# RWKV mixer: the inverse of each chunk's 64-row triangle from two 32-row substitutions and a joining product

## The chip, the cores and the metric

The kernel runs on one core of a Trainium2 chip. The metric is the device time of one execution in microseconds (us). The core's engines work side by side, each through its own queue of instructions: PE (TensorE, matrix products and transposes), DVE (VectorE), ACT (ScalarE), POOL (GpSimd), and SP, whose queue here issues nearly all DMA transfers. An instruction that waits for another engine or for a transfer holds everything behind it on its own engine.

## What is computed

One step of a hybrid decoder layer for a prompt of 512 tokens and a sample group of 8 x 8 tokens (576 columns in all), width 2048. One large projection `x @ w_in` feeds four mixers: RWKV-7, sliding-window attention, mLSTM and retention. Each mixer's output is gated and projected, the four are summed with sigmoid gates, one output projection and a layer norm follow. All in float32. The RWKV mixer has 16 heads of 64 channels and is, token by token:

```python
def step(S, inp):
    r_t, w_t, k_t, v_t, kk_t, a_t = inp
    sa = jnp.einsum('bhvk,bhk->bhv', S, -kk_t)
    S = (S * w_t[:, :, None, :] + sa[..., None] * (kk_t * a_t)[:, :, None, :]
         + v_t[..., None] * k_t[:, :, None, :])
    return S, jnp.einsum('bhvk,bhk->bhv', S, r_t)
```

Since `sa` of a token depends on the updates of the tokens before it, a chunk of 64 tokens worked at once needs the solution of a unit triangular system of 64 rows, I + M1, for each head. The kernel makes the (transposed) inverse of that triangle and multiplies with it.

## The kernel before

**Phases.** Phase 1 makes the projections and runs the four mixers one after another, RWKV (`branch_a`) first. Phase 2 makes the branch projections, phase 3 the output projection and the norm.

**The order on PE.** Projections of phase 1 are one stream. A projection is 16 steps (`dense_steps`), each of six products: the weights' and the inputs' exact high and low parts (`wh`, `wl`, `xh`, `xl`), three combinations by two column groups. `pump(n)` puts n steps into the program between a mixer's own instructions; those that a mixer asked for come first, then gates and other projections that nothing waits for. PE's instructions keep the program's order (`InOrder`), and so do POOL's. Instructions of DVE and ACT stay behind the last weight split before them (`Behind`). The splits of weights into `wh` (ACT, L1280) and `wl` (DVE, L1281) and the loads into the three `raw` buffers (SP, L1297) belong to the stream. `paced` keeps a DMA issue behind PE's work so far in the order in which the program is laid out; it is no wait at run time.

**RWKV.** Two heads (a pair) at a time, eight pairs, 9 chunks of 64 tokens each; the ninth is the sample group. For pair j+1, `prepare` makes keys, decays and the norm of the keys: their squares are summed on PE, `nr` is raised to the power -1/2 on POOL, and DVE copies it out for a transpose (`e<-nr`, `nb<-nr`). `grams` makes the chunk's products, masks them (`m1`, the tile tag `e3`) and starts the inversion. `recur` runs the chunks in order: each solve multiplies with the inverse `TT` (in the profile `TTbd`). The order is `grams(j)`, `prepare(j+1)`, 34 steps, `recur(j)`, `grams(j+1)`; before the last `recur` stand 110 steps.

**The inversion.** The 18 triangles of a pair (2 heads by 9 chunks) are stored to DRAM with one triangle per row (`m1d`, L435 and L436), and loaded seven times over, once for each of `NG` = 7 groups, so that 126 partitions hold (group, triangle) (`MU`, L443). Group g has the unknowns' rows g, g+7, g+14 and so on, ten of them (`NJ` = 10). `invert` is then a forward substitution on POOL: for each of 63 rows i one product `tmp = TU[:, :, i] * MU[i]` and one difference `TU -= tmp`, over i//7+1 of a partition's rows and 63-i columns. The result goes to DRAM (`td`, L385) and comes back with rows on partitions (`TTbd`, two loads, L390). `invert` is a generator: with each `pump` step it moves on one `yield`, so its instructions are spread over the projection steps: `ROWS_BEFORE` steps before the first row, one step a row and one more after every fifth, then `ROWS_STORE`, `ROWS_LOAD` and `ROWS_AFTER` steps around the two transfers. `recur` first takes steps until the generator has ended.

```python
S.paced(S.nc.sync.dma_start(out=td.rearrange("c a g t -> g c a t"), in_=tu[0:n]))
...
nc.sync.dma_start(out=mu[0:18 * NG], in_=m1d.unsqueeze(0).broadcast_to([NG, 18, 3072]))
S.side.append(self.invert(st, mua, mub, tu, tmp))
```

Lines that recur in the profile: L1177 is the helper that keeps the order of PE and POOL, L1193 the one of DVE and ACT; so groups are told apart by their tiles.

Of the kernel before, what the change touches and what calls it, by code (L numbers as in the profile page):

```python
# [13 lines left out]
ALU = mybir.AluOpType  # L14
# [17 lines left out]
# steps of a projection before the next one's first weights, and before its result is stored  # L32
AHEAD = 15
STORE = 6
# weights that are loaded between the pieces of x
# [53 lines left out]
def _constants():  # L89
    """Tables that depend on shapes alone."""  # L90
# [18 lines left out]
    g, jj = i // 18, np.arange(10)  # L109
    c["tinit"] = (np.arange(64)[None, None] == (g[:, None] + 7 * jj[None])[:, :, None]).astype(f).reshape(P, 640)  # L110
# [37 lines left out]

CONST = _constants()
# [4 lines left out]
NG = 7  # L154
NJ = 10
# steps of the projections put between the steps of this branch
# [11 lines left out]
# the pace of the inversion's rows, in such steps  # L168
ROWS_BEFORE = 8
ROWS_PACE = 5  # L170
ROWS_STORE = 4
ROWS_LOAD = 4
ROWS_AFTER = 3


def shift_mix(S, pool, ps, col, out, result):
    """token shift: x + (previous x - x) mu"""
# [39 lines left out]
class RwkvBranch:  # L217
    """Two heads at a time, in chunks of 64 tokens; the ninth chunk is the sample group.

    Rows of the arrays of a head pair: the even head's channels (or tokens) lie on partitions  # L220
    0..63 and the odd head's on 64..127; `ri` names the half that is not the head's own."""
# [6 lines left out]
    def __init__(self, S, pool):  # L228
# [7 lines left out]
        t = lambda name, shape: pool.tile([P] + shape, FP32, name=name)  # noqa: E731  # L236
# [27 lines left out]
    def ask(self, j):  # L264
        """the projections of a pair: keys, receptances and values (with 64 zeros on both sides)"""
        S = self.S

        def finish(n, col):
            def f(ps):
                if n == "v":  # L270
                    x = self.tile("xv", (T + 128,))
                    S.V.memset(x[:, 0:64], 0.0)
                    S.V.memset(x[:, 64 + T:], 0.0)
                    return shift_mix(S, self.pool, ps, col, x[:, 64:64 + T], x)
                x = self.tile("x" + n)
                return shift_mix(S, self.pool, ps, col, x, x)
            return f

        for n, col in (("k", 8 + j), ("r", j), ("v", 16 + j)):
            S.ask(f"a_{n}{j}", finish(n, col), 256)  # L280

    def prepare(self, j):
# [4 lines left out]
        # normalised keys  # L287
# [14 lines left out]
        # decay and learning rate  # L302
# [10 lines left out]
        # running sums of the decays' logarithms  # L313
# [31 lines left out]
        # bonus of the current token  # L345
# [14 lines left out]
        for h in range(2):  # L360
            rs = self.HALF[h]
            ch = lambda x: x[rs].rearrange("p (c t) -> p c t", c=9)  # noqa: E731
            stt(bk[rs, :, h], ch(t2), -0.5, ch(di))
            tt(bk[rs, :, 1 - h], ch(k), ch(di))
        self.st[j] = dict(r=r, kk=kk, bk=bk, bo=bo, dl=dl, vx=vx)

    def invert(self, st, mua, mub, tu, tmp):
        """forward substitution, one row of the unknowns' right side after another"""
        S, n = self.S, 18 * NG
        for _ in range(ROWS_BEFORE):  # L370
            yield 1
        for i in range(63):
            a = min(i // NG + 1, NJ)
            w = 63 - i
            row = mua[0:n, i, i + 1:64] if i < 32 else mub[0:n, i - 32, i - 31:32]
            S.tt(tmp[0:n, 0:a, 0:w], tu[0:n, 0:a, i:i + 1].to_broadcast([n, a, w]),
                 row.unsqueeze(1).to_broadcast([n, a, w]), eng=S.G)
            S.tt(tu[0:n, 0:a, i + 1:64], tu[0:n, 0:a, i + 1:64], tmp[0:n, 0:a, 0:w], ALU.subtract, eng=S.G)
            if i % ROWS_PACE == ROWS_PACE - 1:
                yield 1  # L380
            yield 1
        for _ in range(ROWS_STORE):
            yield 1
        td = S.dpool.tile([18, NJ, NG, 64], FP32, tag="td", name="td", bufs=2)
# [4 lines left out]
        for h in range(2):  # L389
            S.paced(S.nc.sync.dma_start(out=TT[self.HALF[h], :, h],  # L390
                                        in_=td[9 * h:9 * h + 9].rearrange("c a g t -> (a g) c t")[0:64]))
        for _ in range(ROWS_AFTER):
            yield 1

    def grams(self, j):
# [3 lines left out]
        for h in range(2):  # L399
            rs = self.HALF[h]  # L400
            ch = lambda x: x[rs].rearrange("p (c t) -> p c t", c=9)  # noqa: E731
            act(Z[rs, :, h, 0], ch(st["kk"]))
            act(Z[rs, :, h, self.SLOT_R[h]], ch(st["r"]))
        # products of the chunk's tokens, masked
# [4 lines left out]
        for c0, n in ((0, 4), (4, 4), (8, 1)):  # L409
# [7 lines left out]
            for h in range(2):  # L417
# [4 lines left out]
                b1 = lambda x: x.unsqueeze(1).to_broadcast([64, n, 64])  # noqa: E731  # L422
# [8 lines left out]
        # inverse of I + M1, transposed: rows (group, head, chunk), each group every seventh row  # L431
        m1d = S.dpool.tile([18, 3072], FP32, tag="m1d", name="m1d", bufs=2)
        for h in range(2):
            d = m1d[9 * h:9 * h + 9]
            nc.sync.dma_start(out=d[:, 0:2048].rearrange("c (i t) -> i c t", i=32), in_=m1[64 * h:64 * h + 32])  # L435
            nc.sync.dma_start(out=d[:, 2048:].rearrange("c (i t) -> i c t", i=32),  # L436
                              in_=m1[64 * h + 32:64 * h + 64, :, 32:64])
        mu = self.tile("MU", (3072,))
        mua, mub = mu[:, 0:2048].rearrange("p (i t) -> p i t", i=32), mu[:, 2048:].rearrange("p (i t) -> p i t", i=32)
        tu = self.tile("TU", (NJ, 64))  # L440
        tmp = self.tile("tmp", (NJ, 64))
        nc.sync.dma_start(out=tu, in_=S.I["c_tinit"].rearrange("p (a b) -> p a b", a=NJ))
        nc.sync.dma_start(out=mu[0:18 * NG], in_=m1d.unsqueeze(0).broadcast_to([NG, 18, 3072]))  # L443
        S.side.append(self.invert(st, mua, mub, tu, tmp))
        # tokens on partitions
# [30 lines left out]
        # the sample group's queries, masked to each batch  # L476
# [9 lines left out]
    def recur(self, j):  # L486
# [12 lines left out]
        two = lambda x: x.rearrange("p a b -> p (a b)")  # noqa: E731  # L499
# [29 lines left out]
        # the sample group  # L529
# [32 lines left out]
        # norm of each head (the even head's tokens on partitions 64..127)  # L562
# [26 lines left out]
def branch_b(S):  # L589
    nc, V, mm, tr, act, tt, stt, pm = S.nc, S.V, S.mm, S.tr, S.act, S.tt, S.stt, S.pm  # L590
    with S.tc.tile_pool(name="brb", bufs=1) as pool:
# [84 lines left out]
        def outputs(j, s):  # L676
            # probabilities with keys on partitions
# [29 lines left out]
        # the sample group: (KV head, query head, token) on partitions  # L707
# [46 lines left out]
def gate_rows(S, pool, dpool):  # L754
    """mLSTM gates, heads on partitions 0..7; returns the per-token rows the heads need"""
# [59 lines left out]
    # rows to every partition, by way of DRAM  # L815
# [4 lines left out]
    # tokens on partitions: [., 0:8] li - F, [., 32:40] weights of the state, [., 64:72] exp(-m)  # L820
# [20 lines left out]
def branch_c_heads(S, fmd, scd, cols):  # L841
    nc, V, mm, act, tt, stt, pm = S.nc, S.V, S.mm, S.act, S.tt, S.stt, S.pm
    with S.tc.tile_pool(name="brc", bufs=1, reuse_waits="tile") as pool:
# [4 lines left out]
        def conv(j, ps):  # L848
            """causal convolution of four taps and silu; twice its value"""
# [38 lines left out]
        for j in range(4):  # L888
# [4 lines left out]
            # row factors on every partition  # L893
# [20 lines left out]
            # keys with tokens on partitions, weighted for the state  # L914
# [23 lines left out]
            for e in range(2):  # L938
                h = 2 * j + e
                rs = slice(64 * e, 64 * e + 64)  # L940
                # weights of the scores, keys on partitions
# [31 lines left out]
                # the sample group  # L973
# [27 lines left out]
def rope(S, pool, ps, cos, sin, half, name, bufs=2):  # L1001
    """x cos + (x with its halves swapped) sin, channels on partitions"""
# [19 lines left out]
def branch_d(S):  # L1022
    nc, V, mm, act, tt, stt, pm = S.nc, S.V, S.mm, S.act, S.tt, S.stt, S.pm
    with S.tc.tile_pool(name="brd", bufs=1) as pool:
# [18 lines left out]
        for h in range(8):  # L1043
# [4 lines left out]
            # queries with their decay  # L1048
# [5 lines left out]
            # keys and values with tokens on partitions  # L1054
# [14 lines left out]
            # scores, keys on partitions  # L1069
# [12 lines left out]
            # outputs, chunk after chunk, and the states  # L1082
# [19 lines left out]
            # the sample group: one state for each batch  # L1102
# [23 lines left out]
def head_out(S, pool, o, i, h, which, den=None):  # L1126
    """norm over the head's 128 values (tokens on partitions), transposed, gain and bias"""
# [35 lines left out]
def hybrid_kernel(ctx: ExitStack, tc: tile.TileContext, I, O):  # L1163
# [3 lines left out]
    class InOrder:  # L1167
        """an engine whose instructions keep the order of the program"""
# [14 lines left out]
    class Behind:  # L1183
        """an engine whose instructions stay behind the last weight split before them"""
# [45 lines left out]
    def paced(ins):  # L1230
        """not before TensorE's work so far"""
# [35 lines left out]
    def behind_x(ins):  # L1267
        """not before the loads of x"""
# [16 lines left out]
    def dense_steps(src, nk, hi, lo, spl=SPL, order=False, first=None):  # L1285
        """[128 columns of src, T] = src^T @ (hi + lo); src [128, nk, 128] in DRAM."""
# [53 lines left out]
    # the projections of phase 1 as one stream, put between the mixers' steps: those that a  # L1340
    # mixer has asked for come first, then those that wait for nothing
# [7 lines left out]
    def step_finish(name, steps):  # L1349
        """one step of what follows a projection; False when it was the last"""  # L1350
# [14 lines left out]
    def start():  # L1365
        """the next projection, its first weights at once"""
# [26 lines left out]
    def duet():  # L1393
        """the first two projections side by side, while x comes in"""
# [20 lines left out]
    # phase 1  # L1415
# [49 lines left out]
    def rstd(pool, var, n, rows=slice(0, P), tag="rstd"):  # L1465
        """(var + eps) ** -0.5 of [rows, n]"""
# [9 lines left out]
    # phase 2: branch projections times their gates, summed in channel-major order  # L1476
# [21 lines left out]
    # the last of the projections cover the loads of the first branch  # L1498
# [8 lines left out]
    for n, i in enumerate(ORDER):  # L1507
        yh, yl = ys
        for c in range(16):
# [13 lines left out]
            if n == 3:  # L1523
                # the sample group's two parts lie side by side: one pass takes both
# [9 lines left out]
    # phase 3: output projection, residual, layer norm; tokens on partitions  # L1534
# [100 lines left out]
def device_inputs(inp):  # L1635
    """The inputs as the program reads them: the same values in another order."""
# [21 lines left out]
    # states: b h v k -> pair, (h k), b, v  # L1658
# [7 lines left out]
    # (h2 d) pair, b, v | n  # L1666
# [19 lines left out]
def returned(r):  # L1686
    """The outputs as the reference has them: the same values in another order."""
# [35 lines left out]
```

## Time and profile before

| | |
|---|---|
| three runs | 3387.62, 3391.55, 3398.9 us; median 3391.55 |
| profiled execution, first to last instruction | 3394.3 us |
| mean granted clock of PE | 0.985 |
| PE busy | 3292.9 us, 24166 instructions |
| DVE, ACT, POOL busy | 1561.2, 993.5, 696.9 us |
| POOL's two instructions of a row | 262.7 and 263.5 us, 504 of each |
| DMA | 384.67 MB, mean 113 GB/s |

The profiled execution is one more execution of the same program; its span is 0.1% above the median. In the profile's groups a line gives the engine, the operation, what is written from what (out<-in), the shapes, the count, then the busy time, the mean of one in ns, and the engine's idle time just before these instructions with what ended it. Timeline rows give start, duration, engine, operation and, in brackets, the idle time before and its releaser. Rows of windows give the stretch, its length, the busy time of PE, weight loads, DVE, ACT and POOL with counts, the mean granted clock of PE, the share of the 16 DMA engines and GB/s.

### The profile page before, as it was taken

How to read it: one execution, taken by the hardware profiler on the slowest of the kernel's cores; microseconds unless marked ns; L12 is line 12 of the kernel's file. 1: busy time of each engine (PE TensorE's matmuls, PEld its weight loads, DVE VectorE, ACT ScalarE, POOL GpSimd, SP SyncE). 2: the span in 40 equal slices, each digit the busy share in tenths (PEclk: the TensorE clock that was granted, in tenths of full speed). 3: DMA queues.
4: the chain of work that ended last, by engine and by line, in shares of the span. 5: the costliest groups of instructions: out<-in, count | busy, mean ns of one | idle time of the engine just before them, and what ended most of it. 6: DMA issues, size and time to landing. Idle time of an engine off the chain costs nothing.

```text
span 3394.3 us, 59113 instructions
## 1 busy us (share of the span) xinstructions
PE 3292.9 (97%) x24166; PEld 3160.5 (93%) x24166; DVE 1561.2 (46%) x3322; ACT 993.5 (29%) x2023; POOL 696.9 (21%) x1133
## 2 busy tenths in 40 slices
PE   8989998999899999999999999999999999999998
PEld 8979998989899899999999999999999999999886
DVE  5534454544444443334653455533343344555435
ACT  4323232323232323223443222222222222222211
POOL 0434435261708071611310000000000000000000
PEclk9989999999999999999999999999999999999999
DMA  5323232323231323334323333233333365554523
GB/s 166 110 82 108 95 115 84 113 89 111 87 106 63 115 91 107 112 101 133 93 90 107 94 96 95 88 123 119 101 102 115 97 197 184 184 171 132 171 79 106
DMA packets 174144, 384.67 MB, mean 113 GB/s; under 512 B 63704, under 2 KB 67544, under 8 KB 172272
## 3 DMA queue, kind: packets, MB, share of 16 engines
q1 hardware_dynamic: 173872, 380.88, 35.5%
q8 instruction: 190, 3.11, 0.4%
q14 instruction: 82, 0.67, 0.1%
HBM read 316.32 MB, written 58.11 MB: 110 GB/s over the span
## 4 chain that ended last, share of the span: by engine, by line
PE 73%; POOL 15%; DMA 6%; issue 3%; DVE 2%; SPq 1%; ACT 0%; POOLq 0%; ACTq 0%; DVEq 0%
PE psd L1177 45%; PE psd L1223 12%; PE pm L1177 10%; POOL TU L1177 7%; POOL tmp L1177 7%; PE pso L1223 6%; DMA MU<-m1d 3%; DMA raw<-in_wi 1%; DMA td<-TU 0%; POOL nr L1177 0%; DMA TTbd<-td 0%; DMA m1d<-e 0%; DMA raw<-in_wo 0%; DVE e L1193 0%; DVE wl L1281 0%
## 5 line engine op out<-in xcount | busy, mean ns | idle before, releaser
L1177 PE MATMUL psd<-xh,wh 128*128 128x288 f32 (+1 forms) x5472 | 1231.2, 306 | 10.1 <-ACT wh L1280 9.7
L1177 PE MATMUL psd<-xh,wl 128*128 128x288 f32 (+1 forms) x5472 | 1182.4, 297 | 31.7 <-DVE wl L1281 31.7
L1177 PE MATMUL psd<-xl,wh 128*128 128x288 f32 (+1 forms) x5472 | 1181.9, 297 | 0.0
L1281 DVE TENSOR_TENSOR wl<-raw,wh 128x512 fp32r<-128x512 f32 x812 | 595.7, 736 | 945.0 <-ACT wh L1280 928.9
L1280 ACT ACTIVATE wh<-raw 128x512 fp32r<-128x512 f32 x812 | 510.9, 631 | 1601.9 <-PE psd L1177 1218.0
L1177 PEld LDWEIGHTS psd<-xh,wl 128*128 128x128 f32 x5472 | 893.3, 190 | 33.7 <-DVE wl L1281 33.7
L1177 PEld LDWEIGHTS psd<-xh,wh 128*128 128x128 f32 x5472 | 883.4, 190 | 41.3 <-issue 14.5
L1177 PEld LDWEIGHTS psd<-xl,wh 128*128 128x128 f32 x5472 | 892.2, 190 | 0.0
L1177 POOL TENSOR_TENSOR tmp<-TU,MU 126x112 f32<-126x112 f32 (+49 forms) x504 | 262.7, 521 | 381.2 <-DMA MU<-m1d 342.9
L1177 POOL TENSOR_TENSOR TU<-TU,tmp 126x112 f32<-126x112 f32 (+49 forms) x504 | 263.5, 523 | 39.5
L1223 PE MATMUL psd<-yl,wh 128*128 128x288 f32 x1024 | 219.5, 295 | 0.0
L1223 PE MATMUL psd<-yh,wl 128*128 128x288 f32 x1024 | 219.4, 295 | 0.0
L1223 PE MATMUL psd<-yh,wh 128*128 128x288 f32 x1024 | 219.3, 295 | 0.0
L1177 POOL TENSOR_TENSOR rstd<-rstd,mhalf 128x5 f32<-128x5 f32 (+1 forms) x24 | 36.0, 1502 | 727.0 <-DVE rstd L1193 727.0
L1223 PEld LDWEIGHTS psd<-yh,wl 128*128 128x128 f32 x1024 | 164.6, 189 | 0.0
L1223 PEld LDWEIGHTS psd<-yh,wh 128*128 128x128 f32 x1024 | 164.6, 189 | 0.0
L1223 PEld LDWEIGHTS psd<-yl,wh 128*128 128x128 f32 x1024 | 164.6, 189 | 0.0
L1177 POOL TENSOR_TENSOR rs<-rs,mhalf 128x1 f32<-128x1 f32 (+1 forms) x5 | 4.5, 901 | 656.5 <-DVE rs L1193 656.5
L1177 POOL TENSOR_TENSOR smp<-Vbd,c_mrow 64x512 f32<-64x512 f32 x16 | 16.6, 1040 | 429.2 <-PE pm L1177 428.6
L1223 PE MATMUL pso<-w3h,mh 128*128 128x512 f32 x260 | 102.6, 395 | 1.4 <-ACT w3h L1193 1.4
L1223 PE MATMUL pso<-w3l,mh 128*128 128x512 f32 x260 | 103.3, 397 | 0.2 <-DVE w3l L1193 0.2
L1177 POOL TENSOR_TENSOR rsw<-rsw,c_sin 128x576 f32<-128x576 f32 x25 | 38.7, 1548 | 306.3 <-DMA rsw<-rx 306.3
(331 smaller groups left out, 2916.6 us busy)
## 6 DMA issues: line engine op xcount, KB each, us to landing
raw<-in_wi SPq DMA_DIRECT2D x342, 512.0 KB
raw<-in_wb SPq DMA_DIRECT2D x64, 512.0 KB
gd<-zs SPq DMA_DIRECT2D x64, 288.0 KB
th<-gd SPq DMA_DIRECT2D x64, 288.0 KB
raw<-in_wo SPq DMA_DIRECT2D x32, 512.0 KB
MU<-m1d SPq DMA_DIRECT2D x8, 1512.0 KB
zsd<-zs SPq DMA_DIRECT2D x32, 288.0 KB
ya<-yd SPq DMA_DIRECT2D x32, 288.0 KB
```

Of the source, the lines that this page charges most:

```text
L1177: ins = f(*a, **k).ins
L1223: PE.matmul(out=out, lhsT=lhsT, rhs=rhs, start=start, stop=stop)
L1280: a = nc.scalar.activation(out=wh, in_=src, func=ACTF.Copy)
L1281: b = nc.vector.tensor_tensor(out=wl, in0=src, in1=wh.bitcast(FP32), op=ALU.subtract)
```

## The change

The triangle of 64 rows is split into two of 32 and the block above the diagonal. Each inverse diagonal block is made by the substitution on POOL, now for 36 triangles of 32 rows: 31 rows in place of 63, `NG` = 3 groups (108 partitions), `NJ` = 11 rows in each. `m1d` has 36 rows of 1024 values, filled by four stores as before; `MU` is loaded three times over; `td` has 36 triangles; four loads bring the diagonal blocks to `TT`. The block above the diagonal stays on the chip: it is copied to `m12`, PE transposes the nine chunks of `TT` (in three groups, each with a copy to `t11` by ACT and DVE), then for each chunk and head one product of `m12` and `t11`, a copy with a change of sign to `g`, one product of `g` and the lower block, and a copy into `TT`. Between these stand `ROWS_JOIN` = 2 steps. The extra step after every fifth row is gone, `ROWS_STORE` is 3 in place of 4, `ROWS_AFTER` 4 in place of 3. Comments are taken out throughout, which moves line numbers and no instruction.

```diff
+HB = 32
+NG = 3
+NJ = 11
-NG = 7
-NJ = 10
...
-ROWS_PACE = 5
-ROWS_STORE = 4
+ROWS_STORE = 3
 ROWS_LOAD = 4
-ROWS_AFTER = 3
+ROWS_AFTER = 4
+ROWS_JOIN = 2
...
-    def invert(self, st, mua, mub, tu, tmp):
-        S, n = self.S, 18 * NG
+    def invert(self, mu, tu, tmp, m12):
+        S, n = self.S, 36 * NG
+        act, mm, tr, pm, V = S.act, S.mm, S.tr, S.pm, S.V
         for _ in range(ROWS_BEFORE):
             yield 1
-        for i in range(63):
+        for i in range(HB - 1):
             a = min(i // NG + 1, NJ)
-            w = 63 - i
-            row = mua[0:n, i, i + 1:64] if i < 32 else mub[0:n, i - 32, i - 31:32]
+            w = HB - 1 - i
             S.tt(tmp[0:n, 0:a, 0:w], tu[0:n, 0:a, i:i + 1].to_broadcast([n, a, w]),
-                 row.unsqueeze(1).to_broadcast([n, a, w]), eng=S.G)
-            S.tt(tu[0:n, 0:a, i + 1:64], tu[0:n, 0:a, i + 1:64], tmp[0:n, 0:a, 0:w], ALU.subtract, eng=S.G)
-            if i % ROWS_PACE == ROWS_PACE - 1:
-                yield 1
+                 mu[0:n, i, i + 1:HB].unsqueeze(1).to_broadcast([n, a, w]), eng=S.G)
+            S.tt(tu[0:n, 0:a, i + 1:HB], tu[0:n, 0:a, i + 1:HB], tmp[0:n, 0:a, 0:w], ALU.subtract, eng=S.G)
             yield 1
         for _ in range(ROWS_STORE):
             yield 1
-        td = S.dpool.tile([18, NJ, NG, 64], FP32, tag="td", name="td", bufs=2)
+        td = S.dpool.tile([36, NJ, NG, HB], FP32, tag="td", name="td", bufs=2)
         S.paced(S.nc.sync.dma_start(out=td.rearrange("c a g t -> g c a t"), in_=tu[0:n]))
         for _ in range(ROWS_LOAD):
             yield 1
         TT = self.TT
         for h in range(2):
-            S.paced(S.nc.sync.dma_start(out=TT[self.HALF[h], :, h],
-                                        in_=td[9 * h:9 * h + 9].rearrange("c a g t -> (a g) c t")[0:64]))
+            for b in range(2):
+                r0, c0 = 64 * h + HB * b, 18 * h + 9 * b
+                S.paced(S.nc.sync.dma_start(out=TT[r0:r0 + HB, :, h, HB * b:HB * b + HB],
+                                            in_=td[c0:c0 + 9].rearrange("c a g t -> (a g) c t")[0:HB]))
         for _ in range(ROWS_AFTER):
             yield 1
+        t11, g = self.tile("t11", (9, HB)), self.tile("g12", (9, HB))
+        up = (slice(0, HB), slice(64, 64 + HB))
+        down = (slice(HB, 64), slice(64 + HB, P))
+        for c0, m in ((0, 4), (4, 4), (8, 1)):
+            ps = pm()
+            for c in range(m):
+                tr(ps[:, c * P:c * P + P], TT[:, c0 + c].rearrange("p a b -> p (a b)"), S.ident)
+            pv = ps[:, 0:m * P].rearrange("p (c t) -> p c t", c=m)
+            act(t11[up[0], c0:c0 + m], pv[up[0], :, 0:HB])
+            V.tensor_copy(out=t11[up[1], c0:c0 + m], in_=pv[up[1], :, 64:64 + HB])
+            yield 1
+        for _ in range(ROWS_JOIN):
+            yield 1
+        ps = [pm() for _ in range(2)]
+        for c in range(9):
+            for h in range(2):
+                mm(ps[h][down[h], HB * c:HB * c + HB], m12[up[h], c], t11[up[h], c])
+        two = lambda x: x.rearrange("p c t -> p (c t)")
+        act(two(g[down[0]]), ps[0][down[0], 0:9 * HB], scale=-1.0)
+        V.tensor_scalar(out=two(g[down[1]]), in0=ps[1][down[1], 0:9 * HB], scalar1=-1.0, scalar2=None, op0=ALU.mult)
+        for _ in range(ROWS_JOIN):
+            yield 1
+        ps = [pm() for _ in range(2)]
+        for c in range(9):
+            for h in range(2):
+                mm(ps[h][up[h], HB * c:HB * c + HB], g[down[h], c], TT[down[h], c, h, HB:64])
+        for h in range(2):
+            pv = ps[h][up[h], 0:9 * HB].rearrange("p (c t) -> p c t", c=9)
+            if h == 0:
+                act(TT[up[h], :, h, HB:64], pv)
+            else:
+                V.tensor_copy(out=TT[up[h], :, h, HB:64], in_=pv)
+        for _ in range(ROWS_JOIN):
+            yield 1
...
-        m1d = S.dpool.tile([18, 3072], FP32, tag="m1d", name="m1d", bufs=2)
+        m1d = S.dpool.tile([36, HB * HB], FP32, tag="m1d", name="m1d", bufs=2)
...
+        m12 = self.tile("m12", (9, HB))
+        act(m12[0:HB], m1[0:HB, :, HB:64])
+        V.tensor_copy(out=m12[64:64 + HB], in_=m1[64:64 + HB, :, HB:64])
...
-        nc.sync.dma_start(out=mu[0:18 * NG], in_=m1d.unsqueeze(0).broadcast_to([NG, 18, 3072]))
-        S.side.append(self.invert(st, mua, mub, tu, tmp))
+        nc.sync.dma_start(out=mu[0:36 * NG].rearrange("p a b -> p (a b)"),
+                          in_=m1d.unsqueeze(0).broadcast_to([NG, 36, HB * HB]))
+        S.side.append(self.invert(mu, tu, tmp, m12))
```

More of the change, by code (lines that the diff above doesn't have):

```diff
@@ L108, in _constants @@
     c["mss"] = np.concatenate([-su * blk, su * blk, iu * blk], 1)
-    g, jj = i // 18, np.arange(10)
-    c["tinit"] = (np.arange(64)[None, None] == (g[:, None] + 7 * jj[None])[:, :, None]).astype(f).reshape(P, 640)
+    g, jj = i // 36, np.arange(NJ)
+    c["tinit"] = (np.arange(HB)[None, None] == (g[:, None] + NG * jj[None])[:, :, None]).astype(f).reshape(P, NJ * HB)
     rm = np.ones((P, T), f)
@@ L430, in grams @@
                     tt(xs[ri], pv[ri, 0], mk[ri, 1:3])
-        m1d = S.dpool.tile([18, 3072], FP32, tag="m1d", name="m1d", bufs=2)
+        m1d = S.dpool.tile([36, HB * HB], FP32, tag="m1d", name="m1d", bufs=2)
         for h in range(2):
[L434 to L441, printed above, removed]
+            for b in range(2):
+                r0, c0 = 64 * h + HB * b, 18 * h + 9 * b
+                nc.sync.dma_start(out=m1d[c0:c0 + 9].rearrange("c (i t) -> i c t", i=HB),
+                                  in_=m1[r0:r0 + HB, :, HB * b:HB * b + HB])
+        m12 = self.tile("m12", (9, HB))
+        act(m12[0:HB], m1[0:HB, :, HB:64])
+        V.tensor_copy(out=m12[64:64 + HB], in_=m1[64:64 + HB, :, HB:64])
+        mu = self.tile("MU", (HB, HB))
+        tu = self.tile("TU", (NJ, HB))
+        tmp = self.tile("tmp", (NJ, HB))
         nc.sync.dma_start(out=tu, in_=S.I["c_tinit"].rearrange("p (a b) -> p a b", a=NJ))
-        nc.sync.dma_start(out=mu[0:18 * NG], in_=m1d.unsqueeze(0).broadcast_to([NG, 18, 3072]))
-        S.side.append(self.invert(st, mua, mub, tu, tmp))
+        nc.sync.dma_start(out=mu[0:36 * NG].rearrange("p a b -> p (a b)"),
+                          in_=m1d.unsqueeze(0).broadcast_to([NG, 36, HB * HB]))
+        S.side.append(self.invert(mu, tu, tmp, m12))
         S.pump(FILL_TOKENS)
```

## The prediction

> **What bounds the kernel now.** I read the page first, for the engines and the chain that ended last.
>
> ```profile
> PE 3292.9 (97%) x24166; PEld 3160.5 (93%) x24166; DVE 1561.2 (46%) x3322; ACT 993.5 (29%) x2023; POOL 696.9 (21%) x1133
> PE 73%; POOL 15%; DMA 6%; issue 3%; DVE 2%; SPq 1%; ACT 0%; POOLq 0%; ACTq 0%; DVEq 0%
> ```
>
> PE is busy for 97% of the span, in one order that the program fixes. So the change can gain only what PE now waits, and everything it adds to PE's queue costs its full length. POOL's 15% of the chain are rows of the inversion through which the chain runs while PE has other work; they are no gain in themselves. Second view: the groups by form on PE, whose idle column says where PE waits.
>
> ```profile
> L1177 PE MATMUL psd<-xh,wh 128*128 128x288 f32 x4416 | 997.2, 307 | 2.1 <-ACT wh L1280 2.1
> L1177 PE MATMUL psd<-xh,wl 128*128 128x256 f32 x528 | 151.2, 286 | 31.7 <-DVE wl L1281 31.7
> L1177 PE MATMUL pm<-rsb,TTbd 128*128 128x64 f32 x144 | 25.9, 263 | 41.0 <-DMA TTbd<-td 23.9 <-DVE rsb L1193 12.7 <-DVE wl L1281 4.5
> ```
>
> Together 74.8 us. Third view: the timeline of the second head pair, PE, POOL, DVE and SP.
>
> ```profile
> 282.63 0.32 SPq L435 DMA_DIRECT2D m1d<-e  x1
> 285.95 0.82 SPq L443 DMA_DIRECT2D MU<-m1d  x1
> 300.12 0.66 POOL L1177 TENSOR_TENSOR tmp<-TU,MU 126x63 f32<-126x63 f32 x1 [36.67 <-DMA MU<-m1d]
> 334.36 1.96 POOL L1177 TENSOR_TENSOR nr<-nr,mhalf 128x10 f32<-128x10 f32 x1
> 336.35 0.69 DVE L1193 COPY e<-nr 128x512 f32<-128x512 f32 x1 [10.23 <-POOL nr L1177]
> 338.11 0.57 PE L1177 MATMUL psd<-xh,wl 128*128 128x256 f32 x2 [3.72 <-DVE wl L1281]
> 378.85 0.80 SPq L385 DMA_DIRECT2D td<-TU  x1
> 383.87 1.32 SPq L390 DMA_DIRECT2D TTbd<-td  x2
> 388.13 0.41 PE L1177 MATMUL pm<-rsb,TTbd 128*128 128x64 f32 x2 [3.29 <-DVE rsb L1193]
> ```
>
> Each pair but the last has two stalls, both POOL's. The next pair's `nr` power stands in POOL's queue behind 60 row instructions; DVE waits for it (10.23), the weight split `wl` stands behind DVE, PE waits 3.72. Then the rows end late, `td` and `TTbd` follow, and PE waits for the triangle (3.29; the engine named is the last by the profile, the cause is the landing, 4.26 after its issue). In the last pair SP, held at the `td` store, lets a weight load be late: the 2.1.
>
> Fourth view, windows: after such a wait PE's clock is half.
>
> ```profile
> 1110.56:1116.60 6.04, 6.04 (x26) 6.01 (x26) 1.48 (x4) 1.82 (x5) 0.00 (x0) 0.50 0.72 268
> 1116.60:1122.60 6.00, 6.00 (x49) 5.49 (x48) 1.64 (x6) 1.29 (x4) 0.00 (x0) 0.99 0.16 54
> 200.00:1470.00 1270.00, 1200.37 (x8990) 1161.42 (x8991) 568.09 (x1298) 376.10 (x806) 518.29 (x929) 0.97 0.32 100
> ```
>
> The first row begins where a wait ended: 26 products in 6 us against 49, so 2.8 us lost behind one wait. Over the branch the mean of 0.97 is about 76 us at half clock, part of it inside the waits. I count 14 waits that are followed by one at 2 us each, 28 us (the 76 us caps it at 36). **What can be gained: 75 + 28 = 103 us.**
>
> **What is removed.** Per pair POOL had 126 row instructions; it gets 62 on 108 partitions. The element counts per partition, (i//3+1)(31-i) summed over 31 rows, make 1991 per operation, 64 each (before 7140, 113 each).
>
> ```profile
> L1177 POOL TENSOR_TENSOR TU<-TU,tmp 126x63 f32<-126x63 f32 x16 | 7.1, 442 | 1.3
> L1177 POOL TENSOR_TENSOR tmp<-TU,MU 126x63 f32<-126x63 f32 x16 | 5.6, 349 | 343.5 <-DMA MU<-m1d 342.9
> L1177 POOL TENSOR_TENSOR tmp<-TU,MU 126x54 f32<-126x54 f32 x8 | 2.4, 294 | 0.6
> ```
>
> At 64 elements one takes 0.29 to 0.44; I take 0.33 with 0.08 between two (0.6/8): 62 x 0.41 = 25.5 us (bounds 23 and 31). The order of PE's projection steps does not change: the old inversion took 94 steps and the new takes 59 of the 111 between the products and the recurrence (100 in the first pair), so no fill is saved or lost. `nr` now stands behind all 62 instructions, but its own input is there only 43 steps after `m1d`, some 38 us, about when they end: that stall goes.
>
> **What is added to PE**, per pair 9 transposes and 36 products of 32x32 by 32, each a pair of instructions in the records. Rows of the nearest shapes:
>
> ```profile
> 268.09 0.60 PE L1177 MATMUL pm<-c_ident,Yn 128*128 128x128 f32 x4
> 268.45 0.51 PE L1177 MATMUL psd<-xh,wh 128*128 128x288 f32 x2
> 268.80 0.43 PE L1177 MATMUL psd<-xl,wh 128*128 128x288 f32 x2
> 1777.24 0.44 PE L1177 MATMUL pm<-ck,bqb 64*64 64x128 f32 x4
> 1777.51 0.29 PE L1177 MATMUL pm<-bkr,bqb 64*64 64x64 f32 x4
> 1777.73 0.54 PE L1177 MATMUL psd<-xh,wh 128*128 128x288 f32 x2
> ```
>
> Four transposes put 0.36 before the next projection product and lengthen its pair by 0.08 (0.51 against 0.43): 0.44; blocks of 4, 4 and 1 make 1.0. Four instructions of 64 columns take 0.22 with the change of shape behind them. For a block of 36 with half the columns I take 0.4 for the changes of shape and 36 x 0.02: 1.2 (bounds 0.8, with the two heads side by side, and 2.4, one after the other at 0.056); two blocks 2.4. Sum 3.4 per pair (2.6 to 5.8), **8 x 3.4 = 27 us.** ACT and DVE get 12 small copies per pair, beside PE's work except where PE waits for them: two joins have two steps (1.6 us) of cover each, and DVE comes out of the `nr` and shift work there; 0.7 per pair (0 to 3), 6 us.
>
> **The new wait.** The old triangle was wanted by the first solve, over 20 steps after its load. The transposes want it four steps after, and PE's queue is in order: every projection and the mixer stand behind the first transpose, and on ACT and DVE the next weight splits behind its copies. So the chain from `m1d` to the landing must beat PE's 50 steps (8 + 31 + 3 + 4 + 4). One step is 0.80 (54 products are nine):
>
> ```profile
> 1161.64 7.20 PE psd L1177 x54
> ```
>
> With the mixer's own products PE comes there 43.9 us after the first `m1d`; that window of the second pair, PE alone, is full and at full clock:
>
> ```profile
> 282.63:326.51 43.88, 43.88 (x343) 1.00 0.41 128
> ```
>
> The chain, from the same zero:
> - `m1d` to the issue of `MU`: 3.3 (285.95 - 282.63), unchanged: four stores as before.
> - `MU`: 14.2 from issue to first row for 1512 KB. In a stretch of another pair's transfer when little else moves, the DMA share is 0.46, 7.4 engines of 16:
>
> ```profile
> 466.00:470.00 4.00, 4.00 (x32) 4.00 (x32) 0.69 (x1) 1.50 (x5) 0.00 (x0) 1.00 0.46 157
> ```
>
>  The sizes of the two transfers of that kind, from the DMA issues:
>
> ```profile
> MU<-m1d SPq DMA_DIRECT2D x8, 1512.0 KB
> td<-TU SPq DMA_DIRECT2D x8, 315.0 KB
> ```
>
>  Seven is the outer count of that copy (NG = 7), so I read 216 KB per engine. The new one has 432 KB with an outer count of 3, 144 KB per engine: 14.2 x 2/3 = 9.4 if all of it scales, 11.8 if half does; 10 (8.5 to 11.8).
> - Rows: 25.5.
> - `td`: 5.0 (383.87 - 378.85) for 1260 pieces of 256 bytes, 180 per engine. New: 1188 of half the size, 396 per engine. By bytes 5.5, by pieces 11; 7.6, as its start does not scale.
> - `TTbd`: 4.26 with two loads, now four shorter ones: 4.8 (4.3 to 6).
>
> 3.3 + 10 + 25.5 + 7.6 + 4.8 = 51.2, so **PE waits 7.3 us** (bounds 1 and 18). In the first and the last pair `MU` follows `m1d` by 5.6 and 4.6 us and PE is there at about 44.9 and 41.5 (no `prepare` work in the last): 8.6 and 11. Sum 6 x 7.3 + 19.6 = 63 us, with the half clock behind each 8 x 2.1 = 17 us.
>
> SP stands at `td` and `TTbd` till about +47; the load behind them is due at step 66, some +58, and three `raw` buffers cover it; without that cover PE would wait a load of 4 to 6 us in each pair.
>
> The Trainium skill ("DMA: Bandwidth & Descriptors", section "Why a DMA increments its semaphore by 16 and not by 1") says that a copy runs on the largest number of engines up to 16 that divides the slowest dimension on both sides. This speaks against the change: 7 becomes 3 in both transfers. The 0.46 agrees with it for 7; no run yet shows 3. By it the sum is the one here; if the seven engines stayed, it would be the first rival's.
>
> **Sum.** -103 + 27 + 6 + 63 + 17 = +10 us. The profiled execution has a span of 3394.3, 0.1% over the median of 3391.55; on the median 3402.
>
> **Rivals.**
> - *The triangle lands in time.* Transfers stay on seven engines: `MU` 62 KB each, 5.5; `td` 4.5, 3.3 + 5.5 + 25.5 + 4.5 + 4.8 = 43.6, and PE does not wait in the six. -103 + 27 + 6 + 4 = -66: 3325. For it: only the 7 is seen. Against: it equals NG, and NG is 3.
> - *Short wait.* Three engines, but rows at 0.29 + 0.08 and fast transfers, 3.3 + 9.5 + 23 + 7 + 4.6 = 47.4: wait 3.5 in the six, 33 in all. -103 + 27 + 6 + 33 + 17 = -20: 3371.
> - *Joins wait on DVE*: 3 us per pair in place of 0.7, +18: 3420. Against: DVE is 46% busy; for: its queue held 10 us of work behind `nr`.
> - *Rows stay slow* (the other way by more): POOL at its old mean of 0.52 + 0.08 gives 37 us, a wait of 18.8 in the six, +94 over the forecast: 3496. It decides beyond rows of 24 us, where gain and loss cancel. For: the old rows beside DVE's bursts took that; against: the new ones run before the bursts.
>
> ```profile
> L1177 POOL TENSOR_TENSOR tmp<-TU,MU 126x112 f32<-126x112 f32 (+49 forms) x504 | 262.7, 521 | 381.2 <-DMA MU<-m1d 342.9
> ```
>
> **How the numbers follow.** Forecast, waits of 5 to 10 us, 3383 to 3425: 0.5. In time 0.14; short wait 0.2; joins 0.11; slow rows 0.05. Within 0.3%, about what a measurement can tell from no change, is 3381 to 3402. Faster: 0.14, 0.17 of the short wait and 0.03 of the forecast, 0.34. Slower: 0.23 of the forecast, 0.11 and 0.05, 0.39. The rest, 0.27, is the same. The range, 3338 to 3432, leaves out most of "in time" and the slow rows.
>
> **What would show it.** Right: `DVE e<-nr` no longer waits for POOL; the solves' idle of 41.0 is gone; PE's idle stands at transposes that read `TTbd`, 50 to 80 us in eight waits, with half clock behind them; `td` to `TTbd` takes 7 to 8 us; POOL's busy time falls to about 340 us (697 - 526 + 8 x 62 x 0.33). Wrong: no idle at the transposes (then 3325), or idle at the 32x32 products instead (the joins), or `MU` landing within 6 us of its issue. An `e<-nr` wait that stays would refute the rows' price.

## The result and the profile after

The changed kernel takes 3422.94 us (median of 4 executions, 3418.84 to 3424.39) against 3390.93 of the kernel before on the same chip (3387.62 to 3398.9): 1.009 times, 95% interval 1.0074 to 1.0107, so 0.9% slower. Its profiled execution has a span of 3421.4 us, 27.1 over the 3394.3 of before, at a mean clock of 0.981. The page after, engines and chain:

```profile
PE 3301.5 (96%) x24814; PEld 3171.2 (93%) x24814; DVE 1552.3 (45%) x3370; ACT 1010.7 (30%) x2071; POOL 366.2 (11%) x621
PE 86%; POOL 6%; DMA 5%; issue 1%; DVE 1%; SPq 0%; ACT 0%; POOLq 0%; DVEq 0%; ACTq 0%
```

POOL's time has nearly halved (696.9 before), and the chain hardly runs through POOL any more; PE is busy for a smaller share than before. The groups by form on PE tell what it waits for now:

```profile
L1217 PE MATMUL pm<-c_ident,TTbd 128*128 128x128 f32 x72 | 19.6, 410 | 95.4 <-DMA TTbd<-td 95.4
L1217 PE MATMUL pm<-rsb,TTbd 128*128 128x64 f32 x144 | 23.7, 246 | 0.0
L1217 PE MATMUL pm<-TTbd,g 32*32 32x32 f32 x288 | 6.1, 192 | 0.0
L1217 PE MATMUL pm<-t,m 32*32 32x32 f32 x288 | 6.1, 192 | 0.0
```

The solves wait for nothing (41.0 before), nor do the 32x32 products. The first transposes of a pair wait for the triangle's landing, 95.4 us in all. Pair two shows how that comes about; here is its timeline, SP, POOL, DVE and PE together (start, duration, operation, idle time before):

```profile
281.17 1.81 SPq L473 DMA_DIRECT2D m1d<-e  x4
285.88 0.35 SPq L1337 DMA_DIRECT2D raw<-in_wi  x1
286.42 0.78 SPq L482 DMA_DIRECT2D MU<-m1d  x1
296.53 0.24 POOL L1217 TENSOR_TENSOR tmp<-TU,MU 108x31 f32<-108x31 f32 x1 [34.55 <-DMA MU<-m1d]
324.78 0.42 PE L1217 MATMUL psd<-xh,wl 128*128 128x256 f32 x2
325.94 1.95 POOL L1217 TENSOR_TENSOR nr<-nr,mhalf 128x10 f32<-128x10 f32 x1
326.01 0.73 SPq L386 DMA_DIRECT2D td<-TU  x1
327.86 2.10 POOL L1217 TENSOR_TENSOR smp<-krs,c_eye 128x512 f32<-128x512 f32 x2
327.93 2.32 DVE L1233 COPY e<-nr 128x512 f32<-128x512 f32 x1 [3.70 <-POOL nr L1217]
332.80 1.92 SPq L393 DMA_DIRECT2D TTbd<-td  x4
336.41 1.09 PE L1217 MATMUL pm<-c_ident,TTbd 128*128 128x128 f32 x4 [11.21 <-DMA TTbd<-td]
342.86 0.76 PE L1217 MATMUL pm<-t,m 32*32 32x32 f32 x36
343.55 0.53 PE L1217 MATMUL psd<-xh,wh 128*128 128x256 f32 x2
```

From the first `m1d` (281.17) PE arrives after 44.0 us, at 325.2, and the triangle after 55.2. And behind the wait, as before, the clock (windows of the same pair: stretch, length, busy PE, PEld, DVE, ACT and POOL with counts, granted clock, DMA share, GB/s):

```profile
327.50:331.00 3.50, 0.00 (x0) 0.00 (x0) 2.45 (x2) 0.00 (x0) 2.46 (x3) 0.72 0.29 36
336.40:339.40 3.00, 2.99 (x15) 2.98 (x15) 0.53 (x2) 1.17 (x3) 0.00 (x0) 0.52 0.46 145
339.40:342.40 3.00, 3.00 (x25) 3.00 (x24) 2.75 (x9) 0.70 (x4) 0.00 (x0) 1.00 0.02 5
```

15 products in the 3 us behind the wait, 25 in the next three. The first row, with a mean of 0.72, says that the half clock begins inside the wait, where it costs nothing: of some 10 us of it, about 3 stand behind it. To count what it costs, I take the time for which PE is busy in the stretches at clock 0.50 of the RWKV branch and put half of it down as lost. In the change these are eight stretches with 34.9 us of busy time, so 17 us; in the trace of before fourteen stretches with 61.8 us, so 31 us.

### The profile page after: what moved, and what is told of

It reads as the page before. It is cut to its first block, busy times and chain, and to the rows that moved or that the text cites. A ratio compares the mean times of both kernels' runs of the same rounds, so it can differ in the third digit from the quotient of the medians.

```text
span 3421.4 us, 60034 instructions
## 1 busy us (share of the span) xinstructions
PE 3301.5 (96%) x24814; PEld 3171.2 (93%) x24814; DVE 1552.3 (45%) x3370; ACT 1010.7 (30%) x2071; POOL 366.2 (11%) x621
## 4 chain that ended last, share of the span: by engine, by line
PE 86%; POOL 6%; DMA 5%; issue 1%; DVE 1%; SPq 0%; ACT 0%; POOLq 0%; DVEq 0%; ACTq 0%
PE psd L1217 57%; PE psd L1263 12%; PE pm L1217 11%; PE pso L1263 6%; POOL TU L1217 3%; POOL tmp L1217 3%; DMA MU<-m1d 2%; DMA td<-TU 2%; DMA TTbd<-td 0%; SPq L393 0%; DMA raw<-in_wo 0%; DVE BN L1233 0%; DMA raw<-in_wi 0%; DVE res L1233 0%; ACT Z L1233 0%
## 5 line engine op out<-in xcount | busy, mean ns | idle before, releaser
L1321 DVE TENSOR_TENSOR wl<-raw,wh 128x512 fp32r<-128x512 f32 x812 | 585.6, 723 | 933.9 <-ACT wh L1320 911.7
L1217 POOL TENSOR_TENSOR tmp<-TU,MU 108x84 f32<-108x84 f32 (+23 forms) x248 | 96.3, 388 | 336.0 <-DMA MU<-m1d 317.3
L1217 PE MATMUL pm<-c_ident,TTbd 128*128 128x128 f32 x72 | 19.6, 410 | 95.4 <-DMA TTbd<-td 95.4
L1217 PEld LDWEIGHTS pm<-c_ident,TTbd 128*128 128x128 f32 x72 | 13.7, 211 | 97.1 <-issue 96.9
L1217 POOL TENSOR_TENSOR TU<-TU,tmp 108x84 f32<-108x84 f32 (+23 forms) x248 | 100.1, 404 | 19.4
```

What stands on the lines that cost most here:

```text
L1217: ins = f(*a, **k).ins
L1321: b = nc.vector.tensor_tensor(out=wl, in0=src, in1=wh.bitcast(FP32), op=ALU.subtract)
```

## The experiments

The theory to test was the prediction's: the change itself gains, and one wait, at the transposes in PE's queue, gives back more. The rivals: that the waiting merely moves to the next step (rival B in the expectations, where named), and that the joining work costs PE much more than its records say.

**The same work, joined 30 steps later.**

```diff
-ROWS_AFTER = 4
+ROWS_AFTER = 34
```

> The changed kernel with ROWS_AFTER 34 in place of 4: the first transpose stands 30 steps (24 us) later in PE's order; nothing else differs. Theory A (PE loses its time at the first transpose, which comes 11 us before the triangle has landed; 95.4 us in eight waits, and some 11 us of half clock behind them): the waits go and no other comes, 3423 - 95 - 11 = about 3317. Rival B (the wait only moves: DVE and ACT hold the joins up, or DVE's wait for nr, 32 us in the changed kernel, which PE does not feel while it waits itself, reaches PE again as it did before): 20 to 60 us of idle at the products or at wl, 3340 to 3380. Rival C (the added work on PE is the larger cost): no more than 30 us are gained.

Measured: 3312.81 us, ratio to the kernel before 0.9765 (0.975 to 0.9779); run again, 3310.79 and 0.9763 (0.975 to 0.9777). One constant is worth 110 us and turns the change into a gain of 2.35%. From the view of its waits on PE (who waits, for what: us in total, times, longest), the largest, which the change has too, and that for `wl`:

```profile
PE psd L1217 <- ACT wh L1320: 7.9, 3, 7.0
...
PE psd L1217 <- DVE wl L1321: 1.3, 2, 0.8
```

No wait is left at the triangle's transposes, the 32x32 products or the solves. So the wait did not move on; it was a matter of place alone. The wait's 95.4 and the 17 behind it make 112, beside the measured 110; the small waits that are new here, 1.3 at `wl` among them, account for the rest.

> late_join once more, as the measure for the two runs beside it: 3309 to 3316.

**Twenty steps instead of four.**

```diff
-ROWS_AFTER = 4
+ROWS_AFTER = 20
```

> The changed kernel with ROWS_AFTER 20 in place of 4: 16 steps (12.8 us) more before the first transpose, against waits of 10.7 to 13.8 us. It then stands among the vector work of prepare (behind the need for the values), where DVE has most to do. Theory A (steps of cover are taken from the wait one for one): the six middle waits, 11.2 to 12.8, go to nothing, the first keeps about 1 us, 3313 to 3322. Rival B (the joins wait for DVE and ACT there, as their copies stand behind the mixer's operations): 2 to 4 us of idle at the 32x32 products in each pair, 3330 to 3350.

Measured: 3316.14 us, 0.9772 (0.9758 to 0.9787), 3 to 5 us above the two measurements with 34 steps. What is left of the waits in question:

```profile
PE pm L1217 <- DMA TTbd<-td: 1.7, 1, 1.7
PE pm L1217 <- DVE bo L1233: 1.6, 1, 1.6
PE pm L1217 <- DVE t L1233: 0.7, 2, 0.6
```

Sixteen steps more at 0.8 us, some 13 us, cover all eight waits but the first pair's, the longest with 13.8, of which 1.7 remain. The other two rows are the joins, both in the first pair (the 1.6 at its third group of transposes, the 0.7 at its products): 2.3 in all with two steps of cover, so they are no bound.

**The joining block left out.** With the late join, `invert` ends behind the loads of the two diagonal blocks, so the block above the diagonal stays zero.

```diff
-        act(m12[0:HB], m1[0:HB, :, HB:64])
-        V.tensor_copy(out=m12[64:64 + HB], in_=m1[64:64 + HB, :, HB:64])
...
-                tr(ps[:, c * P:c * P + P], TT[:, c0 + c].rearrange("p a b -> p (a b)"), S.ident)
...
-                mm(ps[h][down[h], HB * c:HB * c + HB], m12[up[h], c], t11[up[h], c])
...
-                mm(ps[h][up[h], HB * c:HB * c + HB], g[down[h], c], TT[down[h], c, h, HB:64])
...
```

> As late_join, but the joining part is left out: no m12, no transposes of TT, no 32x32 products and none of their copies, so the block above the diagonal of the inverse is left zero and y_prompt, y_sample and the RWKV state are those of a system without it. Against late_join this is the price of the joining work alone where nobody waits. Theory A: 9 transposes (1.3 us with the changes of shape) and two blocks of 36 at 0.8 us each a pair, 8 x 2.8 = 20 to 23 us: about 3296. By the prediction's bounds 21 to 46 us. If late_join and this one are equal, the joining work is hidden.

Measured: 3290.17 us, 0.9697 (0.9683 to 0.9712). Against the late join's 3312.81 the joining work costs 22.6 us, 2.8 per pair. In the timeline above a block of 36 instructions begins about 0.1 later than a projection product would, holds up the next projection by 0.69 (342.86 to 343.55) and lengthens it by 0.1 (0.53 against 0.43): 0.9, two blocks 1.7 to 1.8 per pair.

**The transposes taken off PE.** With the late join, DVE transposes the 32x32 blocks.

```diff
-                tr(ps[:, c * P:c * P + P], TT[:, c0 + c].rearrange("p a b -> p (a b)"), S.ident)
...
+        for h in range(2):
+            V.transpose(out=t11[up[h]], in_=TT[up[h], :, h, 0:HB])
```

> late_join with the nine transposes on PE and their six copies replaced by two 32x32 block transposes on DVE straight from TT to t11. Theory A (the joining costs what it adds to PE's queue, 22.6 us by late_join less late_no_join, of which the transposes are some 1.3 us a pair): 3313 - 10 = about 3303. Rival: the transposes are hidden in PE's pipeline and only the products cost: 3311 to 3315. If DVE becomes the bound there: idle at the products and 3315 to 3325.

Measured: 3303.2 us, 0.9735 (0.9717 to 0.9753), 9.6 under the late join's 3312.81 and 7.6 under its 3310.79, which was measured on the same chip: nine transposes and the copies around them cost PE 1.0 to 1.2 per pair. With 1.7 to 1.8 for the two blocks of products that makes about the 2.8 of the run before.

**The same transfers on more engines.** Both transfers with an outer count of 3 are issued as three, one for each group, with an outer count of 36; the join stands where the change has it.

```diff
-        S.paced(S.nc.sync.dma_start(out=td.rearrange("c a g t -> g c a t"), in_=tu[0:n]))
+        for q in range(NG):
+            S.paced(S.nc.sync.dma_start(out=td[:, :, q], in_=tu[36 * q:36 * q + 36]))
...
-                          in_=m1d.unsqueeze(0).broadcast_to([NG, 36, HB * HB]))
+        for q in range(NG):
+            nc.sync.dma_start(out=mu[36 * q:36 * q + 36].rearrange("p a b -> p (a b)"), in_=m1d)
```

> The changed kernel with MU loaded by three DMAs (36 partitions from m1d each) and td stored by three DMAs (36 partitions each), so that the outer dimension of each is 36 and not 3; the place of the transposes is that of the changed kernel. Theory A with the transfers on three engines as they are: MU from issue to first row falls from 10.1 to about 7, td to the first TTbd issue from 6.8 to about 4.5, the wait of 11.9 a pair to about 6.5: 3423 - 8 x 5.4 = about 3380. Rival: the transfers are not bound by the number of engines: MU and td take as long as now or longer (more issues on SP), the wait stays at 11 to 13, 3423 or a little more.

Measured: 3369.24 us, 0.9933 (0.9918 to 0.9947). Its group of transposes, and the second pair's timeline:

```profile
L1218 PE MATMUL pm<-c_ident,TTbd 128*128 128x128 f32 x72 | 18.9, 396 | 42.1 <-DMA TTbd<-td 42.1
```

```profile
279.13 1.13 SPq L484 DMA_DIRECT2D MU<-m1d  x3
285.85 0.24 POOL L1218 TENSOR_TENSOR tmp<-TU,MU 108x31 f32<-108x31 f32 x1 [31.16 <-DMA MU<-m1d]
315.74 2.53 SPq L387 DMA_DIRECT2D td<-TU  x3
320.02 1.84 SPq L394 DMA_DIRECT2D TTbd<-td  x4
```

`MU` takes 6.7 from issue to first row in place of 10.1 (286.42 to 296.53), `td` 4.3 in place of 6.8 (326.01 to 332.80): 5.9 per pair, and the waits fall from 95.4 to 42.1, 6.7 per pair. The same bytes went faster; besides the outer count, only the number of issues is another. The Trainium skill ("DMA: Bandwidth & Descriptors", section "Why a DMA increments its semaphore by 16 and not by 1") has the number of engines as the largest up to 16 that divides the slowest dimension on both sides, 3 for the change and 12 here. The traces agree, in every pair: each `MU` and `td` counts up its semaphore once within 1.5 us of the issue, and then, as its data land, seven more times in the kernel before, three in the change and twelve for each part here. A fourfold number of engines saved only a third. For `td` one reason is visible: its three parts are issued 0.9 apart (315.74, 316.64, 317.52), and each lands 2.3 to 2.5 after its own issue. No run has one issue on twelve engines, so what the engines and what the three issues do is not separated.

**The same split where PE does not wait**, with the late join, twice.

> late_join with MU and td in three DMAs each, as in spread. Theory A: with the cover in place the triangle lands long before its transposes, so what the transfers take is hidden: no change from late_join, 3309 to 3317. Rival: the transfers cost something beside the first wait (weight loads held back behind td on SP, DMA engines kept busy): 5 to 15 us faster than late_join.

> late_spread once more beside late_join on one chip. Its trace has no wait on PE that late_join lacks or loses, so theory A (hidden transfers are worth nothing) expects the intervals of the two to overlap, a difference under 4 us; the rival, that the transfers cost something beside the wait, expects 4 to 8 us in favour of this one again.

Measured: 3308.01 us, 0.9749 (0.9735 to 0.9764), and 3308.57, 0.9753 (0.974 to 0.9767), beside 3312.81 and 3310.79 of the late join: 2 us in the same call and 5 across two chips, with overlapping intervals. The split that was worth 54 us at the wait (3422.94 - 3369.24) is worth next to nothing where 30 steps hide it. With the DVE transposes as well:

> The transposes on DVE, the first use of the triangle 30 steps later and the transfers in three DMAs each. Theory A: as dve_transpose, 10 us under late_join of the same call, about 3303; the rival of the run before adds its 4 to 8 us, about 3297.

Measured: 3301.01 us, 0.9733 (0.972 to 0.9746), the lowest time here, and not told apart from the 3303.2 without the split.

**The old stalls, one at a time.** In the kernel before, the power -1/2 of `nr` is taken off POOL:

```diff
-        G.tensor_tensor(out=nr, in0=nr, in1=S.mhalf[:, 0:10], op=ALU.pow)
+        act(nr, nr, ACTF.Sqrt)
+        V.reciprocal(out=nr, in_=nr)
```

> The kernel before with nr made by a square root on ACT and a reciprocal on DVE in place of the power on POOL, so that it does not stand behind POOL's rows; the inversion is the old one. Theory A (31.7 us of PE's idle at wl come from nr's place in POOL's queue, with about 11 us of half clock behind them): 3390 - 43 = 3347, if the rest stays where it is; if the other stall grows by what the pair gains before it (PE comes to the solve earlier, the rows end when they did), most of it is lost again: 3370 to 3390. Rival: nr was not the cause, DVE comes no earlier: 3385 to 3395.

Measured: 3378.96 us, 0.9959 (0.9944 to 0.9974). The two groups that had 31.7 and 41.0:

```profile
L1178 PE MATMUL psd<-xh,wl 128*128 128x256 f32 x528 | 148.7, 282 | 0.3 <-DVE wl L1282 0.3
L1178 PE MATMUL pm<-rsb,TTbd 128*128 128x64 f32 x144 | 26.2, 265 | 69.8 <-DVE rsb L1194 52.6 <-DMA TTbd<-td 17.2
```

The first stall is gone and the second took 29 of its 31 us: PE came to the solves earlier, POOL's rows did not end earlier. The idle time at the two fell by 2.6 us only; what the half clock costs fell, by the count above, by 10 (40.7 us of busy time at 0.50 in place of 61.8, in eight stretches in place of fourteen). Together that is most of the 14.1 between the profiled spans (3394.3 and 3380.2). The two stalls were largely one lateness, that of POOL's rows, met in two places.

**The kernel before with more steps ahead of the recurrence.**

```diff
-FILL_RECUR = 34
+FILL_RECUR = 54
```

> The kernel before with FILL_RECUR 54 in place of 34: the recurrence of each pair but the last, and so the first use of its triangle, stands 20 steps (16 us) later; the inversion is the old one. Theory A (of the 103 us that the old inversion cost, the part at the solves is only a matter of place): the 41 us at the solves fall to what the last pair shows (2 us each, weights behind td), with half of the half clock: 3391 - 41 + 14 - 14 = about 3350; the 31.7 us at wl behind nr stay. Rival: SP, held at td until the rows end, keeps the weight loads back, and PE waits as long for these: no gain, 3385 to 3395.

Measured: 3403.24 us, 1.0039 (1.0023 to 1.0055). Its waits on PE, and SP's queue in the second pair:

```profile
PE psd L1177 <- ACT wh L1280: 36.4, 9, 8.7
PE psd L1177 <- DVE wl L1281: 32.1, 8, 8.3
PE psd L1223 <- ACT yh L1193: 10.5, 4, 7.2
```

```profile
373.32 0.33 SPq L1297 DMA_DIRECT2D raw<-in_wi  x1
390.62 0.80 SPq L385 DMA_DIRECT2D td<-TU  x1
395.53 1.80 SPq L390 DMA_DIRECT2D TTbd<-td  x2
397.43 0.57 SPq L1297 DMA_DIRECT2D raw<-in_wi  x1
```

The solves wait in the last pair alone (5.1, before which the steps are as they were); the weight splits wait instead: 36.4 for `wh` (9.7 before), and the 32.1 for `wl` stay. The next weight load stands in SP's queue behind `td`, which waits for POOL's rows, and behind `TTbd`: 24 us between two loads. PE also waits 10.5 for `yh`, at the start of phase 2; that the stream of projections is used up earlier would explain it, and is not shown. So these 20 steps did not hide the old substitution, while 16 hid the short one. This is what the change is worth.

## Why the prediction was right, and where its terms were off

Right in sign and within its range, 21 us short of the median. The sign owes something to luck: the prediction gave a slower kernel 0.39 and a faster one 0.34. The way in which the time is lost, eight waits at the transposes, was foreseen.

**What can be gained, 103.** Right: both old stalls are gone, 74.8 us, and the half clock behind them cost 31 by the count above, 106 together. The late join without the joining block is 100.3 us below the kernel before (3390.43 - 3290.17).

**The `nr` stall.** Wrong as put: the prediction had `DVE e<-nr` no longer waiting for POOL, and a wait that stays as a refutation of the rows' price. The view of the waits on `nr`, before and after:

```profile
POOL nr L1177: 78.0, 7
```

```profile
POOL nr L1217: 32.1, 7
```

DVE still waits 4.6 on average in seven pairs, 3.70 in the second, where the rows ended 1.7 us later than `nr`'s input was there and the power itself takes 1.95. PE hardly feels it: nothing at `wl` in the change, and in the late join, where no wait at the transposes covers it, the 1.3 shown there. What failed here was the test, not the rows' price alone: a wait need not be zero to be covered.

**What is added to PE, 27.** Measured 22.6. The blocks of products, put at 1.2 within 0.8 and 2.4, took 0.9, near the lower end; the transposes, put at 1.0 a pair, 1.0 to 1.2 with their copies.

**The joins, 6.** Measured none: no idle time at the products in the change, 2.3 with 20 steps. *Joins wait on DVE* falls.

**The new wait, 63.** The mechanism and its place were right, eight waits at the transposes; the term was mis-sized, 95.4. PE's arrival, 43.9, came at 44.0. The chain, predicted and measured in the second pair:

| step | predicted | measured |
|---|---|---|
| `m1d` to `MU`'s issue | 3.3 | 5.25 |
| `MU` | 10 | 10.1 |
| rows | 25.5 | 29.5 |
| `td` | 7.6 | 6.8 |
| `TTbd` | 4.8 | 3.6 |
| sum | 51.2 | 55.2 |

Two of the five were low. "Unchanged: four stores as before" failed, though the stores are the same. A weight load stands in SP's queue between `m1d` and `MU` in both kernels. Before, it went out right behind the stores:

```profile
284.56 0.42 SPq L1297 DMA_DIRECT2D raw<-in_wi  x1
```

In the change it goes out at 285.88 only: SP waits for the split `wl` (285.12 to 285.82), which DVE now does behind its new copy to `m12` and other copies, while before it was done at 284.22. `MU` waits behind that load. And a row instruction took 0.39 and 0.40 where the prediction had 0.33:

```profile
L1217 POOL TENSOR_TENSOR tmp<-TU,MU 108x84 f32<-108x84 f32 (+23 forms) x248 | 96.3, 388 | 336.0 <-DMA MU<-m1d 317.3
L1217 POOL TENSOR_TENSOR TU<-TU,tmp 108x84 f32<-108x84 f32 (+23 forms) x248 | 100.1, 404 | 19.4
```

The two 63-element rows that the prediction shows, 0.349 and 0.442, have a mean of 0.396, which with its 0.08 between two gives 29.5 us, the measured time; the 0.33 was taken below its own nearest rows. The difference goes with DVE's work: in the trace of the change 310 of the 496 row instructions run while DVE is idle, 0.30 on average, and 186 while it works, 0.55. In the last pair, without `prepare` on DVE, the new rows took 27.0 from the first row to the store. The prediction had counted on rows that "run before the bursts". This is also why POOL stands at 366.2 and not at 340. *Rows stay slow* saw this with too high a price (0.52), *short wait* had it the wrong way.

**Three engines.** *In time* needed `MU` in 5.5; it took 10.1, on three engines by its semaphore counts, and in three parts on twelve it took 6.7. The prediction read its seven engines, which the counts of before confirm, off a DMA share of 0.46. The same reading fails for the change: while little but `td` moves (the row 327.50 to 331.00 above), the share is 0.29, which would be 4.6 engines of 16, and three count.

**The half clock, 17.** Measured 17, by the count above.

With the measured terms: -74.8 - 31 + 95.4 + 17 + 22.6 = +29, beside the 27.1 between the spans. So the forecast came nearer than its largest new term: the wait was put 32 us too low, and in part this was offset by chance, as the added work and the joins were put 10 us too high together and the gain 3 too low.

## What to carry to other kernels

Where work is moved onto the engine that bounds the kernel, ask where in its queue it reads what is late: the gain here was real, 2.35%, but was given back whole by a consumer that came some 15 steps (11.9 us) too early in an engine that keeps its order. Price the chain that leads to such a consumer with rows taken beside the neighbours that it will really have, its queue as well as its engine, and then leave a margin of the size of the error (here 4 us in 51, against a wait that nothing covered). And two waits of one engine for the same late producer are not two gains: taking one away hands its time to the other.

## What the runs showed of the hardware

- **36 small instructions in 0.69 us.** 18 products of 32x32 by 32 columns, two instructions each, which take the two heads in turn and so two parts of the array, took 0.69 us: 19 ns an instruction. In the records the starts lie 7 and 25 ns apart in turn. The Trainium skill ("TensorE: Matmul & The Clock Gate", section "Wait — 56ns, not 53.3ns?") has about 25 ns from start to start as the least for a small product; every second step of this block is under that, so here the row decides. No run sends these products without the change of heads, so whether that matters is not shown.
- **A copy on DVE took 2.32 us in place of 0.69.** `e<-nr`, 128x512, took 0.69 beside POOL's rows before; after the change it starts with POOL's two `smp` products of the same size (327.86 to 329.96) and ends just behind them, at 330.25. The run with the split transfers bears this out: of the same six copies there, three lie beside one `smp` and take 1.30 (the one at 494.18, for instance), three beside two and take 2.32. No run took `smp` away.
- **A third, not three quarters.** From an outer count of 3 to one of 36, `MU` went from 10.1 to 6.7 us and `td` from 6.8 to 4.3; `TTbd`, four small loads with sixteen counts each, took 3.6 from issue to use.
